# Sliding-window matmul: PSUM as four tiles of two banks, emptied two banks at a time

## The chip, the cores and the metric

The kernel runs on one core of a Trainium2 chip. The metric is device microseconds (us) of one execution. The kernel before takes 182.0 us.

## The reference

```python
B, S, D, W = 4, 4096, 4096, 64          # x [B, S, D], w [D, D], offsets [B]
for b in range(B):
    o = int(offsets[b])
    results.append(x[b, o:o+W] @ w)     # 64 rows of x by all of w
```

So 256 rows of x are multiplied by one 4096 x 4096 fp32 matrix. Reading w, 67.1 MB, is most of the traffic.

## The kernel before

The four windows form two groups `g` of 128 rows. Weights are cast to fp16 by the loads (issued on POOL) into three rotating buffers `wc` of four row blocks each. PE transposes x through PSUM, then works in three stages: row blocks (all 4096 columns, four or three k-rows at a time; their sums go from PSUM into `acc`), two "column phases" (half of the columns, many k-rows), and the last k-rows of the remaining half. PSUM is eight tiles of one bank (512 fp32 columns) each.

```python
ps = [psum_pool.tile([P, NT], fp32, name=f"bank{t}") for t in range(8)]

def whole_rows(kts, cols, first):              # a row block
    for g in range(G):
        for c in cols:
            bank = n_bank % 8
            n_bank += 1
            for i, kt in enumerate(kts):
                mm(bank, g, kt, src[kt](c * NT, (c + 1) * NT), i == 0, i == len(kts) - 1)
            add_out(bank, g, c)                # acc += bank, on DVE
# ... first block: copies by DVE and ACT in turn ...

def columns(ng, kts):                          # a column phase
    for ki in kts:
        for g in range(G):
            for j in range(n_sub):             # n_sub = 4, bank 4 * g + j
                tail_mm(ki, g, ng, j, ki == kts[0], ki == kts[-1])
    for g in range(G):
        for j in range(0, n_sub, 2):           # even banks by DVE, odd ones by ACT
            add_out(4 * g + j, g, ng * n_sub + j)
            nc.scalar.copy(out=tmp[2 * g + j // 2][:], in_=ps[4 * g + j + 1][:])
    # ... then acc += tmp on DVE

columns(order[1], list(join))                  # first column phase
columns(ng, list(join) + list(range(k_tail, n_k)))   # second; this half is then finished
for g in range(G):
    store(nc.gpsimd, g, ng * NG, (ng + 1) * NG)      # two stores of 1 MB
# ... last k-rows of the other half: eight adds, four stores of 0.5 MB
```

## Time and profile before

| | before |
|---|---|
| time, median | 182.0 us |
| span of the profiled run | 180.2 us |
| PE, DVE, ACT busy | 127.2, 90.6, 18.3 us |
| DVE instructions | 136 |
| moved, rate over the span | 75.5 MB, 419 GB/s |

Busy time is a sum over stages with different limits.

A wait of PE inside a run of matmuls can be hard to see: the ends of matmuls are modelled and overlap, so a PE that is held for 0.2 us still shows as one piece without a gap. The weight loads (PEld) show it. In an unheld run one load takes 0.10 us and one starts every 0.22 us, so loads stand 0.115 us apart; a larger gap is a hold. The kernel before, PEld row of the timeline, across the change from the first column phase to the second, has one merged piece (start, length, count):

```profile
149.03 5.49 PEld L150 LDWEIGHTS <-xT 128*128 128x128 f16 x26
...
164.42 3.14 PEld L150 LDWEIGHTS <-xT 128*128 128x128 f16 x16 [1.26 <-DMA wc<-in_w_dram]
```

The second line is the wait for weights at the start of the last stage. By this row it is 1.26 - 0.115 = 1.15 us. PE's own row, which the prediction reads, shows only 0.77 of it; holds must be compared with the 1.15, as both are then read in the same way.

This is the DMA when weights end and stores begin, in stretches (PE, PEld, DVE, ACT, POOL busy, granted clock, DMA share, GB/s):

```profile
167.00:168.00 1.00, 1.00 (x6) 0.49 (x5) 0.06 (x1) 0.00 (x0) 0.53 (x1) 1.00 1.16 283
168.00:169.00 1.00, 1.00 (x7) 0.43 (x5) 0.00 (x0) 0.00 (x0) 0.00 (x0) 1.00 1.03 379
```

The rate rises from 283 to 379 GB/s while the share stays above 1. The share can read above 1. Before 145 us it jumps from one microsecond to the next (0.15 at 57 to 58 us, 2.28 at 58 to 59), so single microseconds are read only after 146 us; from there to 167, three of them together are never below 0.97.

### The profile page before, as it was taken

The page shows a single profiled execution, that of the slowest core. Times are in us where ns is not written, and L with a number is a line of the kernel's source. Part 1 is how long each engine was busy: PE and PEld are TensorE (multiplying, and loading weights), DVE is VectorE, ACT ScalarE, POOL GpSimd, SP SyncE. Part 2 cuts the span into 40 slices and gives each one's busy share as a digit, 9 for nine tenths or more (in the row PEclk, how much of TensorE's full clock was granted, in tenths as well). Part 3 has the DMA queues.
Part 4 walks back from the last instruction along what each step waited for, and adds up shares of the span by engine and source line. Part 5 has one row for each costly group of instructions (what it writes and reads, how often), then busy time and mean ns, then how long its engine had stood idle before and what let it go on. Part 6 is the DMA issues. An engine that isn't in the chain of part 4 may idle for free.

```text
span 180.2 us, 1537 instructions
## 1 busy us (share of the span) xinstructions
PE 127.2 (71%) x576; PEld 57.0 (32%) x576; DVE 90.6 (50%) x136; ACT 18.3 (10%) x27; POOL 12.7 (7%) x27
## 2 busy tenths in 40 slices
PE   0000789104999499938996599949999999998900
PEld 0000754001344134403442134414444444443400
DVE  0000678100487347833686147725879966409560
ACT  2412556200000000000000000000000004004000
POOL 4600000000000100010001000020007100001100
PEclk9999999855699979996999569987999999999995
DMA  5999989999998899999989999989999999999995
GB/s 186 316 256 216 276 175 204 236 233 226 233 226 189 175 233 233 235 222 233 196 189 211 233 233 218 229 180 213 224 209 215 195 211 213 216 211 208 372 411 209
DMA packets 4152, 40.98 MB, mean 227 GB/s; under 512 B 434, under 2 KB 434, under 8 KB 2226
## 3 DMA queue, kind: packets, MB, share of 16 engines
q0 software_dynamic: 3280, 36.70, 93.4%
q1 hardware_dynamic: 432, 2.10, 3.2%
q10 hardware_dynamic: 434, 2.10, 2.9%
q8 instruction: 4, 0.07, 0.1%
q14 instruction: 2, 0.02, 0.0%
HBM read 71.30 MB, written 4.19 MB: 419 GB/s over the span
## 4 chain that ended last, share of the span: by engine, by line
DMA 58%; PE 30%; issue 3%; DVE 2%; another core or an unknown queue 1%; POOL 1%; POOLq 1%; DVEq 0%
DMA wc<-in_w_dram 58%; PE bank L150 30%; DVE acc L160 2%; POOL wc L114 1%; POOLq L71 1%; POOL xrow L78 0%; DVEq L259 0%; POOL identity masks.py:197 0%; POOLq L78 0%; POOL w L67 0%; POOLq masks.py:199 0%; POOLq L248 0%
## 5 line engine op out<-in xcount | busy, mean ns | idle before, releaser
L150 PE MATMUL bank<-wc,xT 128*128 128x512 f16 x480 | 115.0, 405 | 24.3 <-DMA wc<-in_w_dram 24.3
L160 DVE TENSOR_TENSOR acc<-acc,bank 128x512 f32<-128x512 f32 x112 | 75.2, 687 | 61.5 <-PE bank L150 60.9
L150 PEld LDWEIGHTS <-xT 128*128 128x128 f16 x512 | 52.1, 103 | 93.8 <-DMA wc<-in_w_dram 27.2
L136 PE MATMUL bank<-identity,xrow 128*128 128x128 f16 x64 | 5.3, 258 | 20.0 <-DMA xrow<-in_x_dram 20.0
L203 ACT COPY tmp<-bank 128x512 f32<-128x512 f32 x8 | 4.1, 599 | 127.5 <-PE bank L150 127.5
L145 DVE CAST xT<-bank 128x512 f16<-128x512 f32 x8 | 5.3, 687 | 21.0 <-PE bank L136 20.9
L95 POOL DMA_DIRECT2D wc<-in_w_dram x8 | 4.3, 540 | 108.1 <-PE bank L150 108.1
L136 PEld LDWEIGHTS <-xrow 128*128 128x128 f16 x64 | 5.0, 124 | 20.1 <-issue 20.1
L150 PE MATMUL bank<-w,xT 128*128 128x512 f16 x32 | 7.1, 379 | 0.0
L175 DVE COPY acc<-bank 128x512 f32<-128x512 f32 x8 | 5.4, 688 | 0.9 <-PE bank L150 0.6
L114 POOL DMA_DIRECT2D wc<-in_w_dram x6 | 3.9, 674 | 17.1 <-PE bank L150 17.1
L147 ACT CAST xT<-bank 128x512 f16<-128x512 f32 x8 | 4.4, 593 | 7.1 <-PE bank L136 7.0
L208 DVE TENSOR_TENSOR acc<-acc,tmp 128x512 f32<-128x512 f32 x8 | 5.0, 682 | 0.0
L177 ACT COPY acc<-bank 128x512 f32<-128x512 f32 x8 | 4.7, 586 | 2.1 <-PE bank L150 1.9
L193 POOL DMA_DIRECT2D out_dram<-acc x2 | 1.1, 538 | 26.6 <-DVE acc L208 26.6
L64 ACT CAST w<-acc 128x2048 f16<-128x2048 f32 x1 | 1.9, 1897 | 4.9 <-DMA acc<-in_w_dram 4.9
L78 POOL DMA_DIRECT2D xrow<-in_x_dram x4 | 2.1, 524 | 2.1 <-issue 2.1
L63 ACT CAST w<-acc 128x2048 f16<-128x2048 f32 x1 | 1.9, 1897 | 2.8 <-DMA acc<-in_w_dram 2.8
L63 ACT ACT_TABLE_LOAD x1 | 1.3, 1283 | 1.8 <-PEq L248 1.8
L67 POOL DMA_DIRECT2D w<-in_w_dram x1 | 0.7, 660 | 0.8 <-POOLq L248 0.8
masks.py:199 POOL TENSOR_SCALAR_AFFINE_SELECT identity<-identity 128x128 f16<-128x128 f16 x1 | 0.3, 290 | 0.1
masks.py:197 POOL MEMSET identity<- 128x128 f16 x1 | 0.2, 224 | 0.0
(4 smaller groups left out, 0.4 us busy)
## 6 DMA issues: line engine op xcount, KB each, us to landing
wc<-in_w_dram POOLq DMA_DIRECT2D x5, 4096.0 KB, 42.1
wc<-in_w_dram POOLq DMA_DIRECT2D x4, 1024.0 KB, 24.6
wc<-in_w_dram POOLq DMA_DIRECT2D x1, 3072.0 KB, 37.1
xrow<-in_x_dram POOLq DMA_DIRECT2D x4, 512.0 KB, 14.5
wc<-in_w_dram POOLq DMA_DIRECT2D x1, 2048.0 KB, 26.6
out_dram<-acc POOLq DMA_DIRECT2D x2, 1024.0 KB, 6.3
acc<-in_w_dram SPq DMA_DIRECT2D x1, 1024.0 KB, 5.1
w<-in_w_dram POOLq DMA_DIRECT2D x1, 1024.0 KB, 12.0
```

The source lines that it names most:

```text
L63: nc.scalar.copy(out=w_one[0][:, :NG], in_=w0_32[:, :NG])
L95: nc.gpsimd.dma_start(out=t[:, base : base + r * N], in_=w[k0 * P : (k0 + r) * P, :].rearrange("(p r) n -> p (r n)", r=r),)
L114: nc.gpsimd.dma_start(out=t[:, pos : pos + n * wd].rearrange("p (t n) -> p t n", t=n), in_=w[ki * P : (ki + n) * P, ng * NG + c0 : ng * NG ...
L136: nc.tensor.matmul(out=ps[t][:, i * P : (i + 1) * P], lhsT=x_cols(g, 4 * t + i), rhs=identity[:], start=True, stop=True,)
L145: nc.vector.tensor_copy(out=dst, in_=ps[t][:])
L147: nc.scalar.copy(out=dst, in_=ps[t][:])
L150: nc.tensor.matmul(out=ps[bank][:], lhsT=xT[g][:, kt * P : (kt + 1) * P], rhs=rhs, start=start, stop=stop,)
L160: nc.vector.tensor_add(out=dst, in0=dst, in1=ps[bank][:])
L175: nc.vector.tensor_copy(out=acc[g][:, c * NT : (c + 1) * NT], in_=ps[bank][:])
L177: nc.scalar.copy(out=acc[g][:, c * NT : (c + 1) * NT], in_=ps[bank][:])
L203: nc.scalar.copy(out=tmp[2 * g + j // 2][:], in_=ps[4 * g + j + 1][:])
L208: nc.vector.tensor_add(out=dst, in0=dst, in1=tmp[2 * g + j // 2][:])
```

## The change

The intent: two neighbouring banks become one tile, so that one instruction of 1024 columns empties what took two of 512. DVE and ACT pay the fixed part of an instruction half as often. The core of the diff, cut at `...` (the transposes and the first block's copies change likewise):

```diff
-    ps = [psum_pool.tile([P, NT], fp32, name=f"bank{t}") for t in range(8)]
+    pairs = [psum_pool.tile([P, 2 * NT], fp32, name=f"banks{t}") for t in range(4)]
+    def banks(b, n=1):
+        return pairs[b // 2][:, b % 2 * NT : (b % 2 + n) * NT]
 ...
-    def add_out(bank, g, c):
-        dst = acc[g][:, c * NT : (c + 1) * NT]
-        nc.vector.tensor_add(out=dst, in0=dst, in1=ps[bank][:])
+    def add_out(bank, n, g, c):
+        dst = acc[g][:, c * NT : (c + n) * NT]
+        nc.vector.tensor_add(out=dst, in0=dst, in1=banks(bank, n))
 ...            # row blocks: both banks of a pair are computed, then
+                    add_out(b0, 2, g, c)
 ...            # column phases
-            for j in range(0, n_sub, 2):
-                add_out(4 * g + j, g, ng * n_sub + j)
-                nc.scalar.copy(out=tmp[2 * g + j // 2][:], in_=ps[4 * g + j + 1][:])
+            add_out(4 * g, 2, g, ng * n_sub)
+            nc.scalar.copy(out=tmp[g][:], in_=banks(4 * g + 2, 2))
 ...            # last adds
-            for j in js:
-                add_out(4 * g + j, g, ng * n_sub + j)
+            add_out(4 * g + js[0], 2, g, ng * n_sub + js[0])
```

More of the change, by code (lines that the diff above doesn't have):

```diff
@@ L52 @@
     w_one = [w1_pool.tile([P, N], fp16, name=f"w1_{i}") for i in range(2)]
-    tmp = [acc_pool.tile([P, NT], fp32, name=f"tmp{i}") for i in range(4)]
+    tmp = [acc_pool.tile([P, 2 * NT], fp32, name=f"tmp{i}") for i in range(G)]
     acc = [acc_pool.tile([P, N], fp32, name=f"acc{g}") for g in range(G)]
-    ps = [psum_pool.tile([P, NT], fp32, name=f"bank{t}") for t in range(8)]
+    pairs = [psum_pool.tile([P, 2 * NT], fp32, name=f"banks{t}") for t in range(4)]
+    def banks(b, n=1):
+        return pairs[b // 2][:, b % 2 * NT : (b % 2 + n) * NT]
     ctx.enter_context(tc.manual_schedule())
@@ L133 @@
     for g in range(G):
-        for t in range(8):
-            for i in range(4):
+        for t in range(4):
+            for i in range(8):
                 nc.tensor.matmul(
-                    out=ps[t][:, i * P : (i + 1) * P],
-                    lhsT=x_cols(g, 4 * t + i),
+                    out=pairs[t][:, i * P : (i + 1) * P],
+                    lhsT=x_cols(g, 8 * t + i),
                     rhs=identity[:],
@@ L142 @@
                 )
-            dst = xT[g][:, t * NT : (t + 1) * NT]
+            dst = xT[g][:, 2 * t * NT : 2 * (t + 1) * NT]
             if t % 2 == 0:
-                nc.vector.tensor_copy(out=dst, in_=ps[t][:])
+                nc.vector.tensor_copy(out=dst, in_=pairs[t][:])
             else:
-                nc.scalar.copy(out=dst, in_=ps[t][:])
+                nc.scalar.copy(out=dst, in_=pairs[t][:])
     def mm(bank, g, kt, rhs, start, stop):
         nc.tensor.matmul(
-            out=ps[bank][:],
+            out=banks(bank),
             lhsT=xT[g][:, kt * P : (kt + 1) * P],
@@ L156, in mm, with whole_rows @@
         )
-    def add_out(bank, g, c):
-        dst = acc[g][:, c * NT : (c + 1) * NT]
-        nc.vector.tensor_add(out=dst, in0=dst, in1=ps[bank][:])
-    n_bank = 0
-    def whole_rows(kts, cols, first):
-        nonlocal n_bank
-        for g in range(G):
-            for c in cols:
-                bank = n_bank % 8
-                n_bank += 1
-                for i, kt in enumerate(kts):
-                    mm(bank, g, kt, src[kt](c * NT, (c + 1) * NT), i == 0, i == len(kts) - 1)
+    def add_out(bank, n, g, c):
+        dst = acc[g][:, c * NT : (c + n) * NT]
+        nc.vector.tensor_add(out=dst, in0=dst, in1=banks(bank, n))
+    n_pair = 0
+    def whole_rows(kts, first=False):
+        nonlocal n_pair
+        for g in range(G):
+            for c in range(0, 2 * n_sub, 2):
+                b0 = n_pair % 4 * 2
+                n_pair += 1
+                for j in range(2):
+                    for i, kt in enumerate(kts):
+                        rhs = src[kt]((c + j) * NT, (c + j + 1) * NT)
+                        mm(b0 + j, g, kt, rhs, i == 0, i == len(kts) - 1)
+                dst = acc[g][:, c * NT : (c + 2) * NT]
                 if not first:
-                    add_out(bank, g, c)
-                elif c % 2 == 0:
-                    nc.vector.tensor_copy(out=acc[g][:, c * NT : (c + 1) * NT], in_=ps[bank][:])
-                else:
-                    nc.scalar.copy(out=acc[g][:, c * NT : (c + 1) * NT], in_=ps[bank][:])
-    whole_rows([0, 1], range(8), True)
+                    add_out(b0, 2, g, c)
+                elif c % 4 == 0:
+                    nc.vector.tensor_copy(out=dst, in_=banks(b0, 2))
+                else:
+                    nc.scalar.copy(out=dst, in_=banks(b0, 2))
+    whole_rows([0, 1], True)
     for k0, r in blocks[2:-n_join]:
-        whole_rows(range(k0, k0 + r), range(8), False)
+        whole_rows(range(k0, k0 + r))
     join = range(blocks[-n_join][0], k_tail)
@@ L200, in columns @@
         for g in range(G):
-            for j in range(0, n_sub, 2):
-                add_out(4 * g + j, g, ng * n_sub + j)
-                nc.scalar.copy(out=tmp[2 * g + j // 2][:], in_=ps[4 * g + j + 1][:])
+            add_out(4 * g, 2, g, ng * n_sub)
+            nc.scalar.copy(out=tmp[g][:], in_=banks(4 * g + 2, 2))
         for g in range(G):
-            for j in range(1, n_sub, 2):
-                c = ng * n_sub + j
-                dst = acc[g][:, c * NT : (c + 1) * NT]
-                nc.vector.tensor_add(out=dst, in0=dst, in1=tmp[2 * g + j // 2][:])
+            c = ng * n_sub + 2
+            dst = acc[g][:, c * NT : (c + 2) * NT]
+            nc.vector.tensor_add(out=dst, in0=dst, in1=tmp[g][:])
     columns(order[1], list(join))
```

## The prediction

> **What bounds the kernel now.** I read the page's 40 slices first, to see which resource is full in every stage, then the chain that ended last, then the stretches where the tensor engine (PE) works, then the end in slices of a microsecond or more.
>
> Slices and HBM total, from the page:
>
> ```profile
> PE   0000789104999499938996599949999999998900
> ...
> DVE  0000678100487347833686147725879966409560
> ...
> DMA  5999989999998899999989999989999999999995
> GB/s 186 316 256 216 276 175 204 236 233 226 233 226 189 175 233 233 235 222 233 196 189 211 233 233 218 229 180 213 224 209 215 195 211 213 216 211 208 372 411 209
> ...
> HBM read 71.30 MB, written 4.19 MB: 419 GB/s over the span
> ```
>
> The DMA row stands at 8 or 9 from the second slice to the last but one. PE and VectorE (DVE) have gaps. The GB/s row doubles at the end: until then the queue reads fp32 weights and writes fp16, so 210 written are 420 read; the last stores move fp32 to fp32. The whole program moves 71.30 + 4.19 = 75.5 MB in 180.2 us, 419 GB/s, and DVE's share of the page (50%) buys nothing by itself.
>
> The chain of work that ended last, in order of time:
>
> ```profile
> 6.86 36.20 DMA wc<-in_w_dram
> ...
> 78.28 42.11 DMA wc<-in_w_dram
> ...
> 137.72 26.65 DMA wc<-in_w_dram
> 164.38 0.04 issue
> 164.42 5.37 PE bank L150 x24
> 169.79 1.57 DVE acc L160 x3
> 171.36 0.19 issue
> 171.55 0.69 DVEq L259
> 172.24 1.79 DVE acc L160 x3
> ```
>
> The chain passes through PE only where a finished row block frees a weight buffer. A load issued then lands 42 us later, though its 4 MB (8.4 MB read) need 20 us at 419 GB/s: it queues behind a whole other block. A buffer freed a microsecond later would not make the DMA engines idle. From 164.42 on compute alone is on the chain; that is the only place where DVE time looks like end time.
>
> PE's stretches, from the timeline filtered to PE:
>
> ```profile
> 62.37 15.61 PE L150 MATMUL bank<-wc,xT 128*128 128x512 f16 x64 [2.57 <-DMA wc<-in_w_dram]
> 81.75 15.67 PE L150 MATMUL bank<-wc,xT 128*128 128x512 f16 x64 [3.77 <-DMA wc<-in_w_dram]
> 101.13 16.70 PE L150 MATMUL bank<-wc,xT 128*128 128x512 f16 x64 [3.71 <-DMA wc<-in_w_dram]
> ```
>
> Every four-row block ends 2.57 to 3.77 us before the next weights land. From 120.43 PE runs 43.22 us without a gap (192 matmuls), then waits only 0.77 us for the weights at 164.42: the thinnest slack of the kernel.
>
> The end, by stretches (engines' busy time, clock, DMA share, GB/s):
>
> ```profile
> 170.00:174.00 4.00, 1.50 (x7) 0.49 (x5) 4.00 (x7) 0.00 (x0) 0.00 (x0) 1.00 0.99 413
> 174.00:177.00 3.00, 0.00 (x0) 0.00 (x0) 0.04 (x1) 0.00 (x0) 0.00 (x0) 0.65 1.02 415
> 177.00:178.00 1.00, 0.00 (x0) 0.00 (x0) 0.00 (x0) 0.00 (x0) 0.00 (x0) 0.50 0.77 307
> 178.00:180.20 2.20, 0.00 (x0) 0.00 (x0) 0.00 (x0) 0.00 (x0) 0.00 (x0) 0.50 0.08 34
> ```
>
> DVE ends at 172.24 + 1.79 = 174.03 and the last 0.52 MB store is issued. After 174.00 the engines still move 3 x 415 + 307 + 2.2 x 34 = 1627 KB (GB/s times us). So some 1.1 MB of earlier stores stood in line, about 2.6 us at 415 GB/s. **The end, too, is set by bytes**; DVE's last add may come about a microsecond earlier or later without the DMA engines running dry.
>
> **What the Trainium skill says.** "DMA: Bandwidth & Descriptors", section "Where 436 GB/s comes from", gives a fabric ceiling of 435 GB/s. The trace agrees: 419 over the span, 96% of it. "VectorE: DVE Perf Modes", section "The TRN2 errata", gives (N+151)/0.96 ns for an fp32 tensor_tensor, 691 ns at 512; this trace has 687. It also says that the fixed latency is paid per instruction, between instructions, which is what the change halves. "ScalarE: Activation LUTs", section "What ACT_TABLE_LOAD costs", gives 186 + 0.833 N ns with immediate scale and bias, 612 ns at 512; the trace has 586 to 599. "PSUM — Partial Sum Buffer", section "PSUM bank collisions raise a hardware error", wants PSUM guarded by bank: PE may not write a bank that is being read. A two-bank read therefore holds both banks for its whole length. No run here shows a collision; in the changed program PE waits once for each pair of banks.
>
> **The change, part by part.** The groups concerned:
>
> ```profile
> L160 DVE TENSOR_TENSOR acc<-acc,bank 128x512 f32<-128x512 f32 x112 | 75.2, 687 | 61.5 <-PE bank L150 60.9
> L145 DVE CAST xT<-bank 128x512 f16<-128x512 f32 x8 | 5.3, 687 | 21.0 <-PE bank L136 20.9
> L203 ACT COPY tmp<-bank 128x512 f32<-128x512 f32 x8 | 4.1, 599 | 127.5 <-PE bank L150 127.5
> L208 DVE TENSOR_TENSOR acc<-acc,tmp 128x512 f32<-128x512 f32 x8 | 5.0, 682 | 0.0
> ```
>
> *DVE.* 136 instructions become 68: adds from PSUM 112 to 56, the three groups of 8 to 4 each. The last eight adds take 4.87 us back to back, so one follows another after (4.87 - 0.687)/7 = 598 ns, 89 ns of overlap. An estimate for 1024 elements by the VectorE formula is 1175/0.96 = 1224 ns long and, with the same overlap, 1135 ns apart. Two old ones cost 1196 apart, so a pair saves 61 ns of DVE time in a row. Busy time, mostly hidden: 68 x 1.224 = 83.2 us against 90.6.
>
> *ScalarE (ACT).* 24 evacuations become 12 of about 586 + 512 x 0.833 = 1013 ns; busy 18.3 to about 17.3 us. Hidden.
>
> *Latency, the other side.* A pair is read only when its second bank is complete. In four-row blocks a pair takes PE 8 x 0.22 = 1.8 us and DVE 1.14, with four pairs to rotate: no wait. In the three-row block 6 x 0.22 = 1.3 against 1.14, still no wait. The transposes and the first two rows end at 32.2, with 10.87 us of waiting before 43.10.
>
> *The tightest spot* is between the two column phases. Before, DVE takes the first bank at 150.09, so PE's last write of that phase is seven matmuls of 0.22 later, 151.64. With pairs, DVE starts the first at 150.31, ends 151.53, starts the second 1.135 after its first start, 151.45, ends 152.67. PE wants that bank at 151.64 + 4 x 0.22 = 152.52: a wait of 0.15, with signalling 0.2 us. ACT's second copy starts about 151.7 and ends 152.7, wanted near 153.2: no wait. With perhaps 0.1 where the first column phase begins, 0.3 us comes out of the 0.77 of slack, so the tail still starts at 164.4.
>
> *The tail.* DVE's first add at 169.16 becomes a pair add one matmul later, 169.38; four pairs end at 169.38 + 3 x 1.135 + 1.224 = 174.01, against 174.03. The saving of 4 x 61 = 0.24 is eaten by waiting for the second bank, 0.22. The half stored earlier finishes its adds about 0.1 us sooner. The bytes are the same, in the same order. **Sum: 0.0 to -0.1 us**, so 182.0 becomes 181.9.
>
> **The rivals.** (1) *DVE is the bound and the saving shows.* For it: DVE is on the chain at the end, full from 170 to 174. If all 61 x 68 ns counted, 4.1 us would go, 177.9. Against it: until 164 PE and DVE wait for weights, and the bytes alone need 75.5 MB / 435 GB/s = 173.5 us. At most the tail's 0.24 us could show: 181.8. (2) *A new PE wait becomes the bound*: two-bank tiles halve the number of separate buffers, from eight to four. If PE loses 1.5 us in the gapless stretch instead of 0.3, the tail starts 0.7 late; the store backlog hides most of that: 182.0 to 182.7. For it: only 0.77 us of slack. Against: DVE needs 1.14 per pair where PE needs at least 1.3. (3) *Crossing a bank boundary costs extra in a read.* At 1.5 us a pair, DVE would lag in the three-row block and in the tail by 4 x 0.37 = 1.5 us: about 183. Nothing in the trace before speaks to it, since no read there spans two banks. (4) *Stores in other order.* The stores' issue times move by under 0.2 us; about 2 us of backlog covers this.
>
> **Range and chances.** The three runs of before lie within 0.12 us, so the range is for the mechanism: 0.6 down (a shorter tail, chance in the DMA rate), 0.8 up (rivals 2 and 3). 2% is 3.6 us. Faster by that would need a higher DMA rate, slower a stall of five times the slack: 0.02 each, 0.96 for within.
>
> **What would show it.** DVE's pair adds at 1.22 us and its busy time near 83; ACT pair copies at 1.01 to 1.04; the DMA row unchanged; PE starting the tail at 164.2 to 164.6 after a wait of some 0.5 us for weights; DVE's last end within 0.2 of 174.0. I am wrong if pair adds take over 1.4 us, if PE waits for DVE over 0.8 us in total after 120, if the tail begins after 165, or if the DMA share falls below 0.9 in any stage before 177.

## The result, and the profile after

The changed kernel takes 182.08 us in the median of six runs (181.96 to 182.76) against 182.01 of the kernel before (181.86 to 182.07): ratio 1.0015, interval 0.9997 to 1.0033. Here and below a ratio is the mean time of one kernel's runs over the mean of the other's of the same rounds, so not quite the ratio of the medians quoted. Executions over 1.5% slower than the fastest of the same kernel are left out of the means.

The instructions did what they were meant to. From the groups of the changed kernel (busy us, mean ns, idle before):

```profile
PE 126.8 (70%) x576; PEld 56.9 (32%) x576; DVE 82.2 (46%) x68; ACT 16.9 (9%) x15; POOL 12.7 (7%) x27
...
HBM read 71.30 MB, written 4.19 MB: 419 GB/s over the span
...
L164 DVE TENSOR_TENSOR acc<-acc,banks 128x1024 f32<-128x1024 f32 x56 | 67.9, 1221 | 69.1 <-PE banks L154 68.5
...
L209 ACT COPY tmp<-banks 128x1024 f32<-128x1024 f32 x4 | 3.9, 1016 | 128.3 <-PE banks L154 128.3
```

DVE lost 8.4 us of work, and its idle time in front of the PSUM adds grew from 61.5 to 69.1 us. Rate and span are as before: what DVE saved, it now spends waiting for PE, and PE waits for weights.

But PE's path is not unchanged. The weight-load row of the changed kernel, in three windows of the timeline, and below it DVE's adds at the same places, from two other windows:

```profile
147.79 2.25 PEld L154 LDWEIGHTS <-xT 128*128 128x128 f16 x11 [0.30 <-issue]
...
151.85 0.74 PEld L154 LDWEIGHTS <-xT 128*128 128x128 f16 x4 [0.30 <-issue]
152.98 1.60 PEld L154 LDWEIGHTS <-xT 128*128 128x128 f16 x8 [0.39 <-issue]
...
164.14 0.10 PEld L154 LDWEIGHTS <-xT 128*128 128x128 f16 x1 [0.27 <-DMA wc<-in_w_dram]
...
165.51 2.04 PEld L154 LDWEIGHTS <-xT 128*128 128x128 f16 x10 [0.39 <-issue]
...
143.92 3.81 DVE L164 TENSOR_TENSOR acc<-acc,banks 128x1024 f32<-128x1024 f32 x3
...
150.57 2.35 DVE L164 TENSOR_TENSOR acc<-acc,banks 128x1024 f32<-128x1024 f32 x2 [2.84 <-PE banks L154]
...
163.11 2.35 DVE L164 TENSOR_TENSOR acc<-acc,banks 128x1024 f32<-128x1024 f32 x2 [7.91 <-PE banks L154]
```

There are four holds where before there is none (147.79, 151.85, 152.98, 165.51). Each ends 0.05 to 0.06 us after a DVE add: the last add of the row blocks at 143.92 + 3.81 = 147.73, the first and second add of the first column phase at 150.57 + 1.22 = 151.79 and 150.57 + 2.35 = 152.92, and the second add of the second phase at 163.11 + 2.35 = 165.46. So PE waits for the fourth pair in the first column phase, for the first and the third pair (the first and the fifth bank) in the second phase, and for the third pair in the last stage. Less the usual 0.115 the holds are 0.19 + 0.19 + 0.28 + 0.28 = 0.9 us. Three of them, 0.65 us, lie ahead of the last stage. There the wait for weights shrank from 1.15 to 0.27 - 0.115 = 0.15 us; the weights were also there 0.28 us sooner in this run (164.14 against 164.42).

Later PE means later stores. The first 1 MB store is issued at 166.9 us instead of 166.2, and the DMA in the same stretches is:

```profile
167.00:168.00 1.00, 1.00 (x6) 0.49 (x5) 0.73 (x1) 0.00 (x0) 0.43 (x1) 1.00 0.82 152
168.00:169.00 1.00, 1.00 (x7) 0.43 (x5) 0.00 (x0) 0.00 (x0) 0.53 (x1) 1.00 1.13 432
```

A small hole, 0.18 of one microsecond below full, stands between the last weights and the first store. This run took 182.01 us, as did the profiled run of the kernel before, so a hole of this size shows no cost. But four of twelve runs of the changed kernel (this set and the repeat below) are at 182.6 to 182.9, though none of 39 of the kernel before is above 182.36. This small thing is what most of the experiments are about.

### The profile page after: what moved, and what is told of

Its sections match the earlier page's. It is cut to its first block, busy times and chain, and to the rows that moved or that the text cites. A ratio compares the mean times of both kernels' runs of the same rounds, so it can differ in the third digit from the quotient of the medians.

```text
span 180.2 us, 1403 instructions
## 1 busy us (share of the span) xinstructions
PE 126.8 (70%) x576; PEld 56.9 (32%) x576; DVE 82.2 (46%) x68; ACT 16.9 (9%) x15; POOL 12.7 (7%) x27
## 4 chain that ended last, share of the span: by engine, by line
DMA 43%; PE 42%; issue 4%; DVE 2%; another core or an unknown queue 2%; POOLq 1%; DVEq 1%; POOL 1%
DMA wc<-in_w_dram 43%; PE banks L154 42%; DVE acc L164 2%; DVEq L263 1%; POOLq L75 1%; POOL xrow L82 0%; POOL identity masks.py:197 0%; POOLq L82 0%; POOL w L71 0%; POOLq masks.py:199 0%; DVEq L164 0%; POOLq L252 0%
## 5 line engine op out<-in xcount | busy, mean ns | idle before, releaser
L154 PE MATMUL banks<-wc,xT 128*128 128x512 f16 x480 | 114.2, 401 | 25.3 <-DMA wc<-in_w_dram 25.1
L164 DVE TENSOR_TENSOR acc<-acc,banks 128x1024 f32<-128x1024 f32 x56 | 67.9, 1221 | 69.1 <-PE banks L154 68.5
L140 PE MATMUL banks<-identity,xrow 128*128 128x128 f16 x64 | 5.5, 264 | 19.6 <-DMA xrow<-in_x_dram 19.6
L209 ACT COPY tmp<-banks 128x1024 f32<-128x1024 f32 x4 | 3.9, 1016 | 128.3 <-PE banks L154 128.3
L149 DVE CAST xT<-banks 128x1024 f16<-128x1024 f32 x4 | 4.8, 1222 | 21.4 <-PE banks L140 21.4
L154 PE MATMUL banks<-w,xT 128*128 128x512 f16 x32 | 7.1, 379 | 0.0
L182 DVE COPY acc<-banks 128x1024 f32<-128x1024 f32 x4 | 4.9, 1225 | 1.6 <-PE banks L154 1.6
L213 DVE TENSOR_TENSOR acc<-acc,tmp 128x1024 f32<-128x1024 f32 x4 | 4.7, 1218 | 0.0
L151 ACT CAST xT<-banks 128x1024 f16<-128x1024 f32 x4 | 4.0, 1014 | 7.3 <-PE banks L140 7.3
L184 ACT COPY acc<-banks 128x1024 f32<-128x1024 f32 x4 | 4.0, 1012 | 3.0 <-PE banks L154 3.0
```

The lines of the kernel that those rows point to most:

```text
L140: nc.tensor.matmul(out=pairs[t][:, i * P : (i + 1) * P], lhsT=x_cols(g, 8 * t + i), rhs=identity[:], start=True, stop=True,)
L149: nc.vector.tensor_copy(out=dst, in_=pairs[t][:])
L151: nc.scalar.copy(out=dst, in_=pairs[t][:])
L154: nc.tensor.matmul(out=banks(bank), lhsT=xT[g][:, kt * P : (kt + 1) * P], rhs=rhs, start=start, stop=stop,)
L164: nc.vector.tensor_add(out=dst, in0=dst, in1=banks(bank, n))
L182: nc.vector.tensor_copy(out=dst, in_=banks(b0, 2))
```

## The experiments

The theories. **Bytes**: the DMA engines are full from start to end, and DVE's saved time is worth nothing. **Its rival**: DVE's time, or its last adds, set the end. **Hole**: the pairs make PE late, stores come late, and a hole in the DMA costs what it lasts. **Its rival**: the line of stores hides a late tail. All times below are of fast runs, 5 or 6 of the edited kernel (4 where said) against 11 of the kernel before; all results were right unless said.

### Is it bytes?

**One load less.** Four runs.

```diff
     for k0, r in blocks[2:]:
+        if k0 == 2:                      # no load; the resident first row instead
+            for q in range(r):
+                src[k0 + q] = src[0]
+            continue
```

> The changed kernel without the load of the first row block (rows 256 to 767 of w, 8.4 MB read); its matmuls and adds stay and take the first resident weights instead, so the result is wrong on purpose. Theory (bytes set the time): 8.39 MB / 419 GB/s = 20.0 us less, 161.5 to 162.7 us. Rival (vector or tensor work sets the time): all that work is still there, so within 5 us of 182.

Measured: 163.13 us against 182.05, ratio 0.8958, 19 us less (wrong result). That is a microsecond short of the forecast: 161.5 to 162.7 was stated, 162.65 to 163.41 came. The bytes fell by 11% (75.5 to 67.1 MB), the time by 10%, and the rate stayed: 417 GB/s over the span against 419. All the PE and DVE work is still there. Bytes set the time; the rival falls.

**More vector work.** Four runs.

```diff
                     add_out(b0, 2, g, c)
+                    if kts[0] < 18:
+                        nc.vector.tensor_add(out=tmp[g][:], in0=dst, in1=dst)
```

> The changed kernel with one more 1024-wide vector add, into a scratch tile, after each pair add of the first four row blocks: 32 adds, 36 to 39 us of DVE work more, DVE busy near 121 us. Theory (DVE is hidden there; a block's 8 x 2.36 = 18.9 us still fit into the 19.3 us between two weight landings): within 0.4 us of the changed kernel. Rival (DVE time counts): up by most of 36 us; half-way rival (PE is slowed through the pairs and weight buffers come free too late): up by 2 to 8 us.

Measured: 182.43 us, ratio 1.0023 (0.4 us) to the kernel before, with DVE busy 118.5 us instead of 82.2. So 36 us of added DVE work cost some 0.4 us (interval 0.1 to 0.75), of which 0.25 is the changed kernel's own difference. That is the change turned round four times over, in the stage where it saves most.

**Two adds in the row blocks.**

```diff
-                    add_out(b0, 2, g, c)
+                    add_out(b0, 1, g, c)
+                    add_out(b0 + 1, 1, g, c + 1)
```

> The changed kernel with two adds of one bank each in place of each pair add of the row blocks (after the pair is complete); DVE busy 48 pairs x (2 x 0.687 - 1.221) = 7 us more, near 90. Theory (the pairs' saving in the row blocks is worth nothing): as the changed kernel within 0.2 us, with the same spread. Rival (the saved DVE time is worth something that the column phases give back): slower by 0.5 us or more.

Measured: 182.05 us, ratio 0.9996 (interval 0.9983 to 1.0009); five runs at 181.74 to 182.19 and one, the profiled one, at 183.1. DVE was busy 85.3 us, not 90: its adds from PSUM are 71.0 us instead of 67.9, since adds that follow closely cost less than twice 0.687. The pair adds of the row blocks bring and cost nothing.

### Do the last adds set the end?

The chain of the kernel before ends in DVE adds. Three runs move the two last adds of the changed kernel.

**Last adds cut short.**

```diff
+            if h == 0:
                 add_out(4 * g + js[0], 2, g, ng * n_sub + js[0])
+            else:                        # two columns in place of 1024
+                c = (ng * n_sub + js[-1]) * NT
+                dst = acc[g][:, c : c + 2]
+                nc.vector.tensor_add(out=dst, in0=dst, in1=banks(4 * g + js[-1])[:, :2])
```

> The changed kernel with the two last adds cut to two columns each (wrong on purpose), so that DVE ends about 2.2 us earlier, near 172.0, and the last two stores are issued 1 to 2.2 us earlier. Theory (a line of stores of about 2.6 us stands before the last one): at most 0.3 us faster, 181.8 to 182.1. Rival (the last adds are on the path that sets the end, as the chain shows): 1.5 to 2.2 us faster, about 180.2.

Measured: 182.06 us, ratio 1.0002 (wrong result). In the profiled run, a slow one (182.82) whose first store came 1.2 us later than the changed kernel's, the last two stores are issued at 173.3 and 173.6, where the changed kernel's 173.1 and 174.2 would have become 174.3 and 175.4. So they leave 1.0 and 1.8 us sooner, and nothing comes of it.

**One, and three, adds in the way.**

```diff
+        for i in range(1 * h):           # 3 * h in the other run
+            nc.vector.tensor_add(out=tmp[0][:], in0=tmp[1][:], in1=tmp[1][:])
         for g in range(G):
             add_out(4 * g + js[0], 2, g, ng * n_sub + js[0])
```

> The changed kernel with one more 1024-wide vector add in front of the two last ones, so that both last stores are issued 1.14 us later. Theory (line of stores): up by 0 to 0.4 us. Rival (chain): up by 1.1 us.

> As the run with one add in the way, but three: both last stores are issued 3.4 us later, at 176.5 and 177.6. Theory (a line of stores of some 2 us beyond what a store needs to start): up by 1.0 to 2.0 us, to 183.1 to 184.2, with a hole in the DMA near 176. Rival (the chain through the last adds sets the end): up by 3.4 us; other rival (stores hide all): no change.

Measured: one add 182.29 us, ratio 1.0010, no more than the changed kernel's own 1.0013 to 1.0015; three adds 183.52 us, ratio 1.0084, so 1.3 us over the changed kernel. The three adds held the last two back by 3.65 us in the trace (from 172.92 to 176.57), not 3.4. The profiled run with three (184.49, one of the two longest) shows where the line of stores ended:

```profile
176.00:177.00 1.00, 0.00 (x0) 0.00 (x0) 1.00 (x2) 0.00 (x0) 0.00 (x0) 1.00 0.73 287
177.00:178.00 1.00, 0.00 (x0) 0.00 (x0) 1.00 (x2) 0.00 (x0) 0.00 (x0) 0.58 0.00 0
```

DVE is busy and the DMA engines stand still. So some 2 us of delay in front of the last stores are free (3.65 less 1.3 by the mean, less 1.9 us by this run, in which 0.27 + 1.00 + 0.67 of the DMA's time is missing from 176 to 179); the prediction's backlog was 2.6. Beyond that, delay costs. Saved DVE time at the end was therefore never to be had.

### Where do the holds come from, and what do they cost?

**The changed kernel again.**

> The changed kernel again, unchanged, in more rounds, so that its difference from the kernel before is known to better than 0.2 us. Two of its six runs were 182.6 and 182.8, all of the kernel before at most 182.07. Theory (the end is set by bytes, and PE's lost slack only makes a small hole in the DMA at 167 to 168 us): 182.1 to 182.3 on average, ratio 1.0005 to 1.0015, with some runs above 182.5. Rival (chance of those runs): ratio within 0.0005 of 1 and no run above 182.3.

Measured: 182.0 us, 181.71 to 182.88, ratio 1.0013 (0.9993 to 1.0034); two of six runs above 182.7. The mean is in the range of the theory and the interval still holds 1; the spread is there again.

**PE late on purpose.**

```diff
                 for j in range(n_sub):
+                    if ng == order[0] and ki == kts[0]:
+                        tail_mm(ki, g, ng, j, True, True)    # made again by the next line
                     tail_mm(ki, g, ng, j, ki == kts[0], ki == kts[-1])
```

> The changed kernel with eight more matmuls (each bank's first product of the second column phase is made twice, the result stays right), so that PE is later by 8 x 0.22 = 1.8 us where no slack is left. Theory (late tensor work opens a hole in the DMA of the same length once the weights have landed at about 167 us): time up by 1.4 to 1.8 us, 183.4 to 183.9, and the DMA share of 167 to 169 us falls below 0.5. Rival, as my prediction had it (the line of stores hides most of a late tail): up by at most 0.6 us, 182.7.

Measured: 183.04 us, 182.75 to 184.23, ratio 1.0076, so 1.1 us over the changed kernel. The eight matmuls made PE less late than the 1.8 us intended: DVE's adds of the second column phase start at 164.58 instead of 163.11, and the first store is issued at 168.4 instead of 166.9, 1.5 us later (the hold at the fifth bank is gone from this run). And:

```profile
167.00:168.00 1.00, 1.00 (x5) 0.46 (x5) 1.00 (x2) 0.00 (x0) 0.00 (x0) 1.00 0.83 154
168.00:169.00 1.00, 1.00 (x7) 0.47 (x5) 1.00 (x2) 0.00 (x0) 0.54 (x1) 1.00 0.19 35
169.00:170.00 1.00, 1.00 (x7) 0.41 (x5) 0.20 (x1) 0.00 (x0) 0.51 (x1) 1.00 0.63 262
```

The shortfall is 0.17 + 0.81 + 0.37 = 1.35 us, of which 0.18 was there already. The cost lies between the two forecasts (1.4 to 1.8, at most 0.6) and agrees with the shortfall of 1.35 - 0.18 = 1.17. So most of the 1.5 us is not hidden by the line of stores: these stores are the ones that form the line. That the last store, not the hole, made the run long can be ruled out: here it is issued at 175.7, in the run with one add in the way at 176.3, and that run took 182.53 us against 183.06.

**Pairs in the row blocks only, and pairs in the column phases only.** The two halves of the change, on tiles of two banks:

```diff
 # the first: column phases bank by bank; last adds likewise
-            add_out(4 * g, 2, g, ng * n_sub)
-            nc.scalar.copy(out=tmp[g][:], in_=banks(4 * g + 2, 2))
+            for j in range(0, n_sub, 2):
 ...            # part = one half of tmp[g]
+                add_out(4 * g + j, 1, g, ng * n_sub + j)
+                nc.scalar.copy(out=part, in_=banks(4 * g + j + 1))
 # the second: row blocks and transposes bank by bank
-                    add_out(b0, 2, g, c)
+                    add_out(bank, 1, g, c)     # after each bank, as in the kernel before
```

> Pairs only in the transposes and the row blocks; the two column phases and the last adds one bank at a time as before. Theory: PE loses 0.2 us instead of 0.87 in its gapless stretch, so it waits about 0.5 us for the weights at 164.4, the last half's first store is issued near 166.2 instead of 166.9, the DMA share at 167 to 168 stays above 1.0, and the time is 182.0 as before, with no runs above 182.3. Rival (the row blocks' pairs cost the slack): PE still without a wait at 164, stores as late as 166.8, time as the changed kernel's.

> The other half: row blocks and transposes one bank at a time, the two column phases and the last adds by pairs. Theory: the waits between column phases are here, so PE loses 0.6 to 0.7 us between 145 and 166, waits at most 0.2 us for the weights at 164.4, and the first store of the last half is issued at 166.6 to 166.9; time as the changed kernel's, 182.0 to 182.3. Rival: PE keeps its 0.7 us of waiting for weights and the stores begin at 166.2.

Measured: 182.79 us (ratio 1.0036) and 215.4 us (ratio 1.1836; the four fast of eight runs, 215.28 to 217.0, the others slow at 218.6 to 220.5). Both forecasts fail, and the second by 33 us. The waits of that run say why (us in total, times, longest):

```profile
PE banks L154 <- DVE acc L164: 37.7, 48, 0.8
```

In these programs a tile is the unit of waiting. While DVE reads one bank of a tile, PE does not write the other, though that one is free; so every pair of the row blocks costs PE 0.8 us and a restart. In the first of the two it is ACT that waits for DVE at a shared tile; its profile has PE 45.34 us from 120.39 for the 192 matmuls that took 43.22, and the first store at 168.5. Part of these 2.1 us is a low clock (0.57 from 120.5 to 127 us, 18 matmuls done instead of 23, about 1.1 us); how much of the time is the shared tile's is not shown. Neither run tells the halves of the change apart, which was their purpose. They show another thing: a tile of two banks must be complete before either bank is emptied. One instruction for both is not needed: the run with two adds after a complete pair lost nothing.

**Single banks for the second row group.** Tiles of two banks for banks 0 to 3, four tiles of one bank for the rest, so no tile is shared by two engines.

```diff
+            if g == 0:
+                add_out(0, 2, g, ng * n_sub)
+                nc.scalar.copy(out=tmp[g][:], in_=banks(2, 2))
+                continue
+            for j in range(0, n_sub, 2):       # banks 4 to 7, one by one
 ...            # part = one half of tmp[g]
+                add_out(4 + j, 1, g, ng * n_sub + j)
+                nc.scalar.copy(out=part, in_=banks(4 + j + 1))
```

> Pairs for the first row group's four banks only (two tiles of two banks), four tiles of one bank for the second group: the column phases and last adds of that group go bank by bank as before, and no tile is touched by two engines. Theory (PE waits at the fifth bank of a column phase because DVE's second pair add frees it too late): PE loses 0.3 us or less in its gapless stretch, waits again 0.4 to 0.7 us for weights at 164.4, stores begin at 166.1 to 166.4, no run above 182.4, mean 182.0. Rival (pairs in the row blocks cost the slack): no wait for weights at 164.4 and runs above 182.5 as in the changed kernel.

Measured: 182.04 us, 181.71 to 182.65, ratio 1.0004 (0.9988 to 1.0019). The weight-load row of this run:

```profile
151.61 2.90 PEld L160 LDWEIGHTS <-xT 128*128 128x128 f16 x14 [0.30 <-issue]
...
164.46 3.14 PEld L160 LDWEIGHTS <-xT 128*128 128x128 f16 x16 [1.10 <-DMA wc<-in_w_dram]
```

One hold of 0.19 us is left, at the first pair of the second column phase; the hold at the fifth bank is gone in both places. PE waits at 164.46 again (0.61 us by its own row; by the load row 1.10 - 0.115 = 0.99, for weights), the first store comes at 166.4, and the DMA share at 167 to 170 is 1.08. So the fifth-bank holds came from the second pair add, as the theory said. But the forecast "no run above 182.4" fails: two runs are at 182.49 and 182.65. So the spread is not explained by the holds alone.

**Stores in quarters.** The changed kernel, with each 1 MB store cut into two that leave as soon as their columns are added.

```diff
             add_out(4 * g, 2, g, ng * n_sub)
+            if ng == order[0]:
+                store(nc.gpsimd, g, ng * NG, ng * NG + 2 * NT)
             nc.scalar.copy(out=tmp[g][:], in_=banks(4 * g + 2, 2))
 ...
             nc.vector.tensor_add(out=dst, in0=dst, in1=tmp[g][:])
+            if ng == order[0]:
+                store(nc.gpsimd, g, c * NT, (c + 2) * NT)
```

> The changed kernel, with each 1 MB store of the half finished first cut in two: 1024 columns of a row group are stored as soon as their pair add is done, near 164.4 and 165.5 us, instead of all 2048 at 166.9 and 168.0. The same bytes. Theory (the slower runs of the changed kernel come from a hole in the DMA at 167 to 169 us, which opens because these stores come late): the hole is filled, share above 1.0 at 167 to 169 even where PE is late, and all runs lie within 181.7 to 182.3, mean 0.2 to 0.3 us below the changed kernel's. Rival (the slower runs come from PE or chance): the spread up to 182.8 stays.

Measured: 182.35 us, 182.16 to 182.76, ratio 1.0024 (1.0011 to 1.0037). The profiled run is further evidence for the hole, though only one pair of runs. PE happened to start its long stretch slowly in it, much as in the profiled run of two adds in the row blocks. This is the run of two adds (183.1 us):

```profile
120.50:127.00 6.50, 6.35 (x16) 2.27 (x17) 1.28 (x2) 0.00 (x0) 0.00 (x0) 0.53 1.07 231
167.00:170.00 3.00, 2.96 (x14) 1.36 (x14) 2.26 (x2) 0.00 (x0) 0.99 (x2) 1.00 0.57 153
```

And this the run with stores in quarters (182.16 us):

```profile
120.50:127.00 6.50, 6.50 (x17) 2.42 (x18) 1.22 (x1) 0.00 (x0) 0.00 (x0) 0.54 1.07 231
167.00:170.00 3.00, 3.00 (x15) 1.37 (x14) 2.04 (x2) 0.00 (x0) 1.60 (x3) 1.00 1.07 354
```

The clock granted in 120.5 to 127 us was 0.53 and 0.54, with 16 and 17 matmuls done, where the kernel before had 0.75 and did 23. DVE's first adds of the second column phase come at 164.64 and 164.42, so PE is equally late, to 0.2 us. With stores at 168.4 the DMA stands at 0.57 for 3 us, a shortfall of 1.3 us; with stores from 165.9 on there is no hole, and the run is 0.9 us shorter. Still the forecast for the set fails: no run is below 182.16, and the mean is above the changed kernel's, not 0.2 to 0.3 below. What these smaller stores cost in the other runs stays open, as those runs have no trace.

### The spread, over all profiles

Granted clock from 120.5 to 127 us, first store, DMA share from 167 to 170 us, and the time of that same run:

| run | clock | first store | DMA share | us |
|---|---|---|---|---|
| before | 0.75 | 166.2 | 1.09 | 182.01 |
| single banks for the second group | 0.74 | 166.4 | 1.08 | 182.09 |
| more vector work | 1.00 | 166.7 | 1.03 | 182.03 |
| changed | 0.74 | 166.9 | 1.00 | 182.01 |
| changed, again | 0.74 | 166.9 | 1.01 | 182.07 |
| one add in the way | 0.59 | 167.8 | 0.77 | 182.53 |
| last adds cut short | 0.56 | 168.1 | 0.70 | 182.82 |
| two adds in the row blocks | 0.53 | 168.4 | 0.57 | 183.10 |
| PE late on purpose | 0.74 | 168.4 | 0.55 | 183.06 |
| pairs in the row blocks only | 0.57 | 168.5 | 0.54 | 183.13 |
| stores in quarters | 0.54 | 165.9 | 1.07 | 182.16 |

(The run with three adds in the way has a hole at another place too and is left out; so are the one at 217 us and the one with a load less.) Below a share of 1 time follows the share; between 1.00 and 1.09 it does not move. And the share follows the first store, whatever made it late: a low clock or added matmuls. A low clock in 120.5 to 127 costs PE 1.3 to 1.5 us (16 or 17 matmuls of 0.22 done instead of 23). With the 1.15 us of waiting for weights that the kernel before has, most of that would be absorbed; with 0.15 left, nearly all of it goes to the stores. So the slower runs of the changed kernel would be those with a low clock there. None of its own slow runs was profiled, but the runs with the last adds cut short and with one add in the way are the same program up to the last two adds, and their profiles, at 182.82 and 182.53, have clocks of 0.56 and 0.59 and shares of 0.70 and 0.77. Against it stand the runs above 182.4 with single banks for the second group, where most of the wait for weights is back, and with stores in quarters, where in the profile there is no hole: the spread is not fully explained. Nor is it shown how often the kernel before meets such a clock; its single profile has 0.75. What makes the clock low in one run and not in another stays open too.

## Why the prediction was right or wrong

**Right: what bounds the kernel, and so the time.** 181.9 was forecast, 182.08 came. One load less took 19 of 20 us; 36 us of DVE work more took about 0.4. The forecast gain of up to 0.1 did not come; the mean is 0.25 higher, within the noise.

**Right: the cost of a pair.** 1224 ns were estimated for a DVE add and 1221 came; the four last adds, 4.61 us in a row, are (4.61 - 1.221)/3 = 1.130 us apart, estimated 1.135. ACT: 1013 estimated, 1016 measured for the copies to `tmp`. DVE busy: 83.2 and 82.2. Rival 3, an extra cost for crossing a bank, falls with the first of these.

**Right: the backlog of stores in front of the last one.** "DVE's last add may come about a microsecond earlier or later" held for cutting the adds short and for one in the way; the free delay is nearer 2 us than 1. DVE's last end came at 169.59 + 4.61 = 174.20, inside the "within 0.2 of 174.0".

**Wrong in size: "The tightest spot".** The step took 0.3 us of holds out of 0.77 of slack. The trace has 0.65 us ahead of the tail, and 0.28 more in it, and the wait for weights that remained was 0.15, not "some 0.5". The step counted one hold of 0.2 in the second column phase and 0.1 in the first. Two terms were missed: the first pair of the second column phase (0.19), where the working had DVE's add end at 151.53, in time for PE at 151.64, and the fifth bank of the last stage (0.28), which it does not mention. The one at the fifth bank of the second phase was 0.28, not 0.2, and the one in the first phase 0.19, not 0.1. Of the prediction's own signs of error one came, "if PE waits for DVE over 0.8 us in total after 120" (0.9). The other, a DMA share below 0.9 before 177, came in one microsecond only (0.82 at 167); over 167 to 170 the share is 1.00.

**Wrong: "The half stored earlier finishes its adds about 0.1 us sooner", and in rival 4 "under 0.2 us" for the stores.** These adds ended at 165.38 + 2.35 = 167.73 instead of 164.57 + 2.49 = 167.06, 0.67 us later, and the first store moved by 0.7. The working carried neither its own holds (0.65 in the trace) nor the wait for the second bank (its 0.22) on to this half; the shorter adds won back 0.27. It did no harm in the profiled run only because the hole that opened is small.

**Wrong in mechanism: rival 2's "the store backlog hides most of that".** For a late PE this fails. The backlog is built by the stores of the first finished half, and they are late with PE. The run with PE late on purpose lost 1.1 us with the first store 1.5 us later. That the predicted time held is to this extent luck: the holds were three times what was forecast, and the kernel before had some slack more than PE's row shows (1.15 instead of 0.77 us).

**Not foreseen: the spread.** The range's upper part, 182.8, was reserved for rivals 2 and 3; single runs did reach it (182.88). Rival 3 is out; whether it was rival 2's route, with the help of the clock, is the inference of the section on the spread and not shown.

No version with a right result beat the kernel before: the best, two adds in the row blocks and single banks for the second group, are at 0.9996 and 1.0004, both with intervals that hold 1.

## What to carry to other kernels

Before merging instructions on an engine, ask who waits for whom: here the saved 8.4 us turned into waiting, because the DMA engines are full from first load to last store. A larger unit of emptying frees its first buffer later, and that shows at phase changes, where the producer wants the first buffers back at once; read it from gaps in the weight loads, as the matmul row hides it. And a backlog hides only lateness behind it: ask whether the late work is itself what builds the backlog.

## What the Trainium skill lacked or had wrong

- "DMA: Bandwidth & Descriptors", section "Where 436 GB/s comes from", says that for transfers between HBM and SBUF the HBM side, about 358 GB/s, is the one that binds. One core alone kept 419 GB/s over a whole span of 180.2 us, and 417 with one load less. The same page's table of single-core measurements has 425, which agrees; the sentence needs its condition.
- The same section's 435 is a ceiling of the ports on the SBUF side. The prediction compares 419 with it, but that counts fp32 bytes read from HBM; the loads write fp16, and the page of the run has 40.98 MB, 227 GB/s, as what the engines moved. No page says which side of a casting load counts, and no run here tells.
- "PSUM — Partial Sum Buffer" gives rules by bank. No page says that in a program of this kind a tile of two banks is waited for as a whole: emptied bank by bank, it cost PE 37.7 us of waits in 48 pairs, and the time went from 182.0 to 215.4 us.
- "ScalarE: Activation LUTs" gives 186 + 0.833 N ns, 1039 ns for 1024 columns; the copies out of two banks took 1012 to 1016. It does not say from which memory its figure is.
- No page gives the cost of an add that reads over a bank boundary ("Advanced Engine Details and Errata" only lists reading several banks with one instruction as possible): 1221 ns, the same as the formula for one operand of that length (1224).
